# A convolution layer whose depthwise convolutions, statistics and element-wise work are laid out anew around the same matmuls

## Chip, cores and metric

One Trainium2 chip, 8 cores, the batch of 16 sequences split two to a core. The metric is the device time of the slowest core in microseconds (us), lower is better. Most executions agree within 0.3%, but an 8-core program also has a slower state in which the cores of one die run at a lower granted TensorE clock.

## The reference, cut to what matters

An encoder of four layers. Layer 1 has the convolution module below; every layer ends in a squared-ReLU MLP.

```python
def conv_module(h, w_in, dw, dw_bias, ln_g, ln_b, w_out):
    val, gate = jnp.split(h @ w_in, 2, axis=-1)
    v = val * jax.nn.sigmoid(gate)                   # (B, S, 1024), S = 2048
    v = depthwise_conv(v, dw, width=31) + dw_bias    # centred, per channel   (shortened)
    mu, var = mean(v), variance(v)                   # over the 1024 channels (shortened)
    vn = (v - mu) * lax.rsqrt(var + LN_EPS) * ln_g + ln_b
    return jax.nn.silu(vn) @ w_out

# ... for each layer i
    x = x + mixers[i](rms_norm(x, norm_mix[i]))
    x = x + sq_relu_mlp(rms_norm(x, norm_mlp[i]), mlp_up[i], mlp_down[i])
```

## The kernel before

A sequence of 2048 positions is cut into four tiles of 512 (`j` = 0 to 3) and the channels into eight chunks of 128 (`c`, or `oc` for outputs). All steps run on TensorE, including the depthwise convolution (32 narrow matmuls with diagonal weights for one chunk of one tile) and the sums over channels (a matmul with a matrix of ones). The matmuls of the trace follow the program's order (22,320 in both), so the order of the calls below is TensorE's schedule. The convolutions come as `conv(0..7)` for tile 0, `8..15` for tile 1, `16..23` for tile 3, `24..31` for tile 2.

```python
def ln_stats(j):                      # mean and reciprocal root of tile j (cut)
    if j > 1:
        flush(j)                      # the ones-matmuls of the tile's last chunks
        b1, b2 = S1, S2               # two fixed PSUM banks
    # ... tiles 0 and 1 use two free banks
    m, r = M[slot[j]], R[slot[j]]     # both in SBUF
    self.act(msq, b1, AF.Square)
    self.copy(m, b1, eng="act")
    self.tt(r, b2, msq, ALU.subtract)
    self.act(r, r, AF.Ln, bias=self.vcol("eps", 1))
    self.act(r, r, AF.Exp, scale=-0.5)

def ln(j, c, lag=2):                  # subtract the mean; two chunks later: scale, swish
    if c < DC:
        C = Cv(c, j)
        self.tt(C, C, M[slot[j]], ALU.subtract, eng="pool" if c % 2 or j == 2 else "dve")
        half.append((j, c))
    while half and (len(half) > lag or c >= DC):
        ln_end(*half.pop(0))

def ln_end(j, c):
    C = Cv(c, j)
    self.tt(C, C, R[slot[j]], ALU.mult)
    self.act(SLv(c, j), C, AF.Silu, bias=..., scale=...)

# ... out(j, oc): 8 matmuls, then x += bank on VectorE, squares on ScalarE for the next norm

for c in range(DC):                   # projection of tile 3
    glu(c, 3)
    if c < 4:
        out(0, 2 * c)
        out(0, 2 * c + 1)
    else:
        self.sq_flush()
    if c > 0:
        conv(7 + c)
    # ...
conv(15)
for c in range(DC):                   # tile 3's convolutions beside tile 1's normalization
    conv(16 + c)
    if c == 0:
        ln_stats(1)
    else:
        ln(1, c - 1)
for c in range(DC):                   # tile 2's convolutions
    conv(24 + c)
    if c == 0:
        ln(1, DC - 1)
        ln(1, DC)
    elif c == 1:
        ln_stats(3)
    else:
        ln(3, c - 2)
    if c % 2:
        out(1, c // 2)
# ... rest of tile 1's output, then tile 3's and tile 2's, each chunk beside ln() and the
# ... operands of the MLP's first products: hsteps() scales the residual (piece) and forms
# ... differences t1 to t4; slot_steps() forms three sums and a difference of weights
```

## Time and profile before

| | before |
|---|---|
| median of the first 3 runs | 4501.51 us (4497.52 to 4760.71) |
| profiled run, slowest core (core 2) | span 4496.5 us |
| spans of its 8 cores | 4476.3 to 4496.5 us, granted clock 0.990 to 0.993 |
| TensorE busy on core 2 | 4347.2 us of 4496.5 |

Two lines of the page's groups of instructions matter later (line, engine, operation, output and input, count, then busy us and mean ns of one, then the idle time before them):

```profile
L351 POOL TENSOR_TENSOR arena<-arena 128x512 f32<-128x512 f32 (+1 forms) x61 | 83.2, 1391 | 964.8 <-ACT arena L348 829.0
L366 DVE CAST arena<-arena 128x512 bf16<-128x512 f32 x32 | 20.4, 638 | 28.1 <-ACT arena L348 26.5
```

The first are GpSimd's subtractions. The second are VectorE's conversions of tiles 2 and 3 for the statistics; a mean of 638 ns hides two populations, which comes up at the end.

### The profile page before, as it was taken

The page shows a single profiled execution, that of the slowest core. Times are in us where ns is not written, and L with a number is a line of the kernel's source. Part 1 is how long each engine was busy: PE and PEld are TensorE (multiplying, and loading weights), DVE is VectorE, ACT ScalarE, POOL GpSimd, SP SyncE. Part 2 cuts the span into 40 slices and gives each one's busy share as a digit, 9 for nine tenths or more (in the row PEclk, how much of TensorE's full clock was granted, in tenths as well). Part 3 has the DMA queues.
Part 4 walks back from the last instruction along what each step waited for, and adds up shares of the span by engine and source line. Part 5 has one row for each costly group of instructions (what it writes and reads, how often), then busy time and mean ns, then how long its engine had stood idle before and what let it go on. Part 6 is the DMA issues. An engine that isn't in the chain of part 4 may idle for free.

```text
span 4496.5 us, 67459 instructions; the slowest of 8 cores (4476.3 to 4496.5 us)
## 1 busy us (share of the span) xinstructions
PE 4347.2 (97%) x22320; PEld 1959.2 (44%) x22320; DVE 2759.3 (61%) x5056; ACT 2020.6 (45%) x3452; POOL 162.7 (4%) x211
## 2 busy tenths in 40 slices
PE   7999999999999999999999999999999999999998
PEld 3444443444444444444444444434444444444443
DVE  2776645876767853677655656456646656426655
ACT  4443435543524445444354434454444344344434
POOL 0000001000010000000000000020000000000000
PEclk9999999999999999999999999999999999999999
DMA  6377755466646664366943445453443244412453
GB/s 158 88 166 197 194 109 123 105 151 206 179 122 158 178 193 128 71 161 194 245 153 108 153 150 148 100 131 115 148 157 143 75 159 150 166 52 101 149 186 132
DMA packets 122741, 652.31 MB, mean 145 GB/s; under 512 B 14624, under 2 KB 55712, under 8 KB 75552
## 3 DMA queue, kind: packets, MB, share of 16 engines
q1 hardware_dynamic: 102240, 517.46, 32.8%
q0 software_dynamic: 20160, 130.56, 16.8%
q8 instruction: 184, 3.01, 0.3%
q14 instruction: 157, 1.29, 0.1%
HBM read 625.35 MB, written 151.07 MB: 173 GB/s over the span
## 4 chain that ended last, share of the span: by engine, by line
PE 86%; DVE 6%; issue 3%; ACT 2%; DMA 2%; SPq 0%; DVEq 0%; POOL 0%; ACTq 0%; POOLq 0%
PE ps L334 86%; DVE arena L351 4%; ACT arena L348 2%; DVE arena L359 2%; DMA arena<-l_pool_w_in 1%; DMA outT<-arena 1%; DMA arena<-scr_v 0%; DMA arena<-scr_mlp 0%; DMA arena<-xT 0%; ACT L348 0%; DVE arena L355 0%; SPq L372 0%; DVEq L285 0%; POOL arena L372 0%; ACT ps L348 0%
## 5 line engine op out<-in xcount | busy, mean ns | idle before, releaser
L334 PE MATMUL ps<-arena 128*128 128x512 bf16 (+4 forms) x22320 | 4347.2, 371 | 131.6 <-ACT arena L348 49.8
L334 PEld LDWEIGHTS ps<-arena 128*128 128x128 bf16 (+1 forms) x22320 | 1959.2, 98 | 2519.1 <-issue 296.1
L351 DVE TENSOR_TENSOR arena<-arena,ps 128x512 f32<-128x512 f32 (+2 forms) x1026 | 721.7, 717 | 784.2 <-PE ps L334 778.1
L351 DVE TENSOR_TENSOR arena<-arena 128x512 bf16<-128x512 bf16 (+4 forms) x2318 | 1102.7, 493 | 161.2 <-ACT arena L348 125.9
L348 ACT ACTIVATE arena<-arena 128x512 bf16<-128x512 f32 (+4 forms) x1239 | 794.6, 652 | 545.4 <-DVE arena L351 513.5
L348 ACT ACTIVATE ps<-ps 128x512 f32<-128x512 f32 x770 | 448.1, 582 | 1100.4 <-PE ps L334 1038.7
L348 ACT ACTIVATE arena<-ps 128x512 f32<-128x512 f32 (+2 forms) x1114 | 614.3, 596 | 541.9 <-PE ps L334 505.0
L359 DVE SCALAR_TENSOR_TENSOR arena<-arena 128x512 bf16<-128x512 f32 (+1 forms) x944 | 666.0, 719 | 99.9 <-ACT arena L348 92.6
L351 DVE TENSOR_TENSOR arena<-ps,arena 128x512 f32<-128x512 f32 x520 | 357.4, 687 | 506.5 <-PE ps L334 474.5
L348 ACT ACTIVATE arena<-ps,arena 128x512 bf16<-128x512 f32 (+2 forms) x294 | 184.5, 664 | 240.2 <-PE ps L334 218.3
L351 POOL TENSOR_TENSOR arena<-arena 128x512 f32<-128x512 f32 (+1 forms) x61 | 83.2, 1391 | 964.8 <-ACT arena L348 829.0
L372 POOL DMA_DIRECT2D arena<-l_mlp x96 | 51.0, 532 | 1720.3 <-PE ps L334 1139.1
L359 DVE SCALAR_TENSOR_TENSOR arena<-arena,ps 128x512 bf16<-128x512 f32 (+1 forms) x75 | 51.2, 694 | 100.2 <-PE ps L334 74.2
L355 DVE TENSOR_SCALAR arena<-arena 128x512 bf16<-128x512 f32 (+1 forms) x112 | 46.5, 462 | 37.4 <-DMA arena<-xT 37.4
L348 ACT ACT_TABLE_LOAD x33 | 42.3, 1283 | 35.8 <-DMA arena<-xT 14.8
L366 DVE CAST arena<-arena 128x512 bf16<-128x512 f32 x32 | 20.4, 638 | 28.1 <-ACT arena L348 26.5
L372 POOL DMA_DIRECT2D arena<-l_conv_w_in x16 | 8.5, 533 | 593.9 <-DVE arena L351 533.1
L369 POOL MEMSET arena<- 128x1024 bf16 (+1 forms) x6 | 4.1, 722 | 471.4 <-DVE arena L351 471.4
L372 POOL DMA_DIRECT2D arena<-l_pool_w_in x14 | 7.6, 560 | 353.4 <-PE ps L334 352.5
L355 DVE TENSOR_SCALAR arena<-ps,arena 128x512 f32<-128x512 f32 x16 | 11.9, 746 | 1.0 <-PE ps L334 0.9
L366 DVE COPY arena<-arena 128x8 bf16<-128x8 bf16 (+1 forms) x10 | 4.0, 405 | 10.2 <-ACT arena L348 9.9
L372 POOL DMA_DIRECT2D arena<-l_conv_w_out x4 | 2.1, 530 | 133.0 <-PE ps L334 133.0
(10 smaller groups left out, 8.0 us busy)
## 6 DMA issues: line engine op xcount, KB each, us to landing
arena<-scr_mlp SPq DMA_DIRECT2D x160, 1792.0 KB, 7.3
scr_mlp<-arena SPq DMA_DIRECT2D x64, 1792.0 KB, 6.7
arena<-l_mlp POOLq DMA_DIRECT2D x96, 1024.0 KB, 8.9
arena<-scr_v SPq DMA_DIRECT2D x256, 130.0 KB, 3.8
arena<-xT SPq DMA_DIRECT2D x32, 512.0 KB, 7.9
outT<-arena SPq DMA_DIRECT2D x12, 1024.0 KB, 5.3
arena<-l_conv_w_in POOLq DMA_DIRECT2D x16, 512.0 KB, 8.4
scr_v<-arena SPq DMA_DIRECT2D x64, 128.0 KB, 2.3
```

The source lines that it names most:

```text
L334: self.P.add("pe", lambda e: e.matmul(out, lhsT, rhs, start=start, stop=stop, skip_group_check=skip), reads=[lhsT, rhs], writes=[out])
L348: self.P.add("act", lambda e: e.activation(out, in_, func, **kw), reads=reads, writes=[out])
L351: self.P.add(eng, lambda e: e.tensor_tensor(out, in0, in1, op), reads=[in0, in1], writes=[out])
L355: self.P.add(eng, lambda e: e.tensor_scalar(out, in0, s1, None, op0), reads=reads, writes=[out])
L359: self.P.add(eng, lambda e: e.scalar_tensor_tensor(out, in0, scalar, in1, op0, op1), reads=reads, writes=[out])
L366: self.P.add(eng, lambda e: e.tensor_copy(out, in_), reads=[in_], writes=[out])
L369: self.P.add(eng, lambda e: e.memset(ap, val), writes=[ap])
L372: return self.P.add(q, lambda e: e.dma_start(out=out, in_=in_), reads=[in_] + list(reads), writes=[out] + list(writes), chan=chan, group=g ...
```

## The change

The intent is to close the places where TensorE waits in the convolution layer. Four parts:

- **Order**: the projection loop of tile 3, which held most of tile 1's convolutions already, takes up to two convolutions a step, so that the first four of tile 3 fit in as well; statistics come earlier, outputs later; queues are one deeper. With it go new bank numbers and a new order of the operand differences behind the last output (the two `rest` lines).
- **Roots**: three reciprocal roots stay in PSUM banks instead of SBUF.
- **Subtractions**: the odd subtractions of tiles 0, 1 and 3 move from GpSimd to VectorE.
- **Tail**: four sums of weights (first sequence) and eight operand differences (each sequence) at the MLP's start move from VectorE to GpSimd.

```diff
-    def hsteps(self, n, pair, gp=()):
+    def hsteps(self, n, pair, gp=(), rs=None):
+        rs = rs or self.RS                     # piece() and root() now use rs[]
...
-        eng = "dve"                            # slot_steps: sums of weights
+        eng = "pool" if i == 0 and KINDS[li] == "conv" else "dve"
...
-        SB = [Rot([self.buf(b, BF16, (TT,), o + i * 1024) for i in range(4)]) for b, o in ((accb, 0), (sgb, 4096))]
+        SB = [Rot([self.buf(7, BF16, (TT,), o + i * 1024) for i in range(4)]) for o in (0, 4096)]
...
-                flush(keep=1)
+                flush(keep=2)
...
-            m, r = M[slot[j]], R[slot[j]]
+            m, r = M[slot[j]], S2 if j == 2 else R[slot[j]]
...
-                self.tt(C, C, M[slot[j]], ALU.subtract, eng="pool" if c % 2 or j == 2 else "dve")
+                self.tt(C, C, M[slot[j]], ALU.subtract, eng="pool" if j == 2 else "dve")
...
-            self.tt(C, C, R[slot[j]], ALU.mult)
+            self.tt(C, C, S2 if j == 2 else R[slot[j]], ALU.mult)
...
-            self.act(self.RS[1], S1, AF.Ln, bias=self.vcol("eps", 0))
-            self.act(self.RS[1], self.RS[1], AF.Exp, scale=-0.5)
+            self.act(S1, S1, AF.Ln, bias=self.vcol("eps", 0))
+            self.act(S1, S1, AF.Exp, scale=-0.5)
...
         for c in range(DC):
             glu(c, 3)
-            if c < 4:
-                out(0, 2 * c)
-                out(0, 2 * c + 1)
-            else:
+            for k in {0: (8,), 4: (15,), 5: (17,), 6: (), 7: (18, 19)}.get(c, (2 * c + 7, 2 * c + 8)):
+                conv(k)
+            if 1 <= c <= 4:
+                out(0, 2 * c - 2)
+                out(0, 2 * c - 1)
+            if c == 4:
+                ...
+                conv(16)
+            elif c == 5:
+                Cb[3] += self.take(9)
                 self.sq_flush()
-            if c > 0:
-                conv(7 + c)
...
-        for c in range(DC):
-            conv(16 + c)
-            if c == 0:
                 ln_stats(1)
-            else:
-                ln(1, c - 1)
+            elif c > 5:
+                for k in (0, 1) if c == 6 else (2, 3, 4, 5):
+                    ln(1, k)
+        for k in (20, 21, 22, 23):
+            conv(k)
+            if k < 23:
+                ln(1, k - 14)
...
         for c in range(DC):
             conv(24 + c)
             if c == 0:
-                ln(1, DC - 1)
-                ln(1, DC)
-            elif c == 1:
                 ln_stats(3)
-            else:
-                ln(3, c - 2)
-            if c % 2:
-                out(1, c // 2)
+            for k in range(c - 1, c) if c else ():
+                ln(3, k)
+            if c in (3, 5):
+                out(1, (c - 3) // 2)
...
+        ln(3, 7)
+        ln(3, DC)
+        out(1, 2)
+        out(1, 3)
+        ln_stats(2)
...
+        r0 = ps[:, 5, :]                       # root of the next norm, in PSUM
+        self.mm(r0, self.cm("ones", 128), nx.sums[0], True, True)
+        self.act(r0, r0, AF.Ln, bias=self.vcol("eps", 0))
+        self.act(r0, r0, AF.Exp, scale=-0.5)
-        for oc in range(5, DC):
+        for oc in range(4, DC):
             out(1, oc)
-            ln(3, oc + 1)
-        ln(3, DC)
-        self.h_open(nx)
+            for k in {4: (0, 1)}.get(oc, (oc - 3,)):
+                ln(2, k)
+        self.h_open(nx, (0, 1), (r0, S1))      # differences of chunks 0, 1 on GpSimd
...
-        rest = [root3] + [h[2 + 8 * k + q] for k in range(4) for q in range(2, 8)]
+        rest = [root3] + [h[2 + 8 * k + q] for k in range(2) for q in range(2, 8)]
+        rest += [h[2 + 8 * k + q] for qs in ((2, 3), (4,), (6,), (5,), (7,)) for k in (2, 3) for q in qs]
...
         for oc in range(DC):
             out(3, oc)
-            ln(2, oc)
-            first.pop(0)()
-        ln(2, DC)
-        self.mlp_sums(s, li)
+            if oc < 3:
+                ln(2, oc + 5)
+            elif oc == 3:
+                ln(2, DC)
+                self.mlp_sums(s, li)
+            else:
+                first.pop(0)()
+                first.pop(0)()
```

More of the change, by code (lines that the diff above doesn't have):

```diff
@@ L723, in load_chunk @@
             self.summed(n, j, n.sums[j])
-    def hsteps(self, n, pair, gp=()):
+    def hsteps(self, n, pair, gp=(), rs=None):
         ja, jb = pair
         h11, h21, h22, t3, t1, t2, t4 = [self.hview(i) for i in range(7)]
+        rs = rs or self.RS
         def piece(dst, kc, half, j, r):
             c = 4 * half + kc
-            self.stt(dst[:, kc, :], self.X[:, c, j * TT:(j + 1) * TT], self.vcol(n.gname, c), self.RS[r],
+            self.stt(dst[:, kc, :], self.X[:, c, j * TT:(j + 1) * TT], self.vcol(n.gname, c), rs[r],
                      ALU.mult, ALU.mult)
-        steps = [lambda: self.root(n, ja, self.RS[0]), lambda: self.root(n, jb, self.RS[1])]
+        steps = [lambda: self.root(n, ja, rs[0]), lambda: self.root(n, jb, rs[1])]
         for kc in range(4):
@@ L745, in hsteps, with h_open @@
         return steps
-    def h_open(self, n, gp=()):
+    def h_open(self, n, gp=(), rs=None):
         if self.hbuilt is not n and self.claim("H"):
             self.hbuilt = n
-            self.htodo = self.hsteps(n, self.pairs[0], gp)
+            self.htodo = self.hsteps(n, self.pairs[0], gp, rs)
     def h_step(self, k):
@@ L1357, in out @@
                 sq3.append((oc, t))
-                sq3_add(2)
+                sq3_add(3)
             if oc == DC - 1:
@@ L1397, in conv_layer @@
             glu(c, 3)
-            if c < 4:
-                out(0, 2 * c)
-                out(0, 2 * c + 1)
-            else:
-                self.sq_flush()
-            if c > 0:
-                conv(7 + c)
-            if c == 3:
-                self.take(slab[0])
-        conv(15)
-        self.rot = Rot([ps[:, i, :] for i in range(6)])
-        Cb[3] = self.take(8, 9)
-        for c in range(DC):
-            conv(16 + c)
-            if c == 0:
-                ln_stats(1)
-            else:
-                ln(1, c - 1)
+            if c == 2:
+                self.take(slab[0])
+            for k in {0: (8,), 4: (15,), 5: (17,), 6: (), 7: (18, 19)}.get(c, (2 * c + 7, 2 * c + 8)):
[4 more added lines that the diff above has]
+            if c == 4:
+                self.rot = Rot([ps[:, i, :] for i in range(6)])
+                Cb[3] = self.take(8)
+                self.take(7)
+                conv(16)
+            elif c == 5:
+                Cb[3] += self.take(9)
+                self.sq_flush()
+                ln_stats(1)
+            elif c > 5:
[5 more added lines that the diff above has]
+                ln(1, k - 14)
         Cb[2] = self.take(10, 15)
@@ L1419, in conv_layer @@
             if c == 0:
-                ln(1, DC - 1)
-                ln(1, DC)
-            elif c == 1:
                 ln_stats(3)
-            else:
-                ln(3, c - 2)
-            if c % 2:
-                out(1, c // 2)
+            for k in range(c - 1, c) if c else ():
+                ln(3, k)
+            if c in (3, 5):
+                out(1, (c - 3) // 2)
         self.release(dgb)
         self.release(v4)
-        self.slots_early(s, li, 2)
-        out(1, 4)
-        ln_stats(2)
-        self.rot = Rot([ps[:, i, :] for i in (0, 1, 2, 3, 4, 5, 7)])
-        for oc in range(5, DC):
+        ln(3, 7)
[3 more added lines that the diff above has]
+        ln_stats(2)
+        self.release(7)
+        self.slots_early(s, li, 2)
+        r0 = ps[:, 5, :]
+        self.rot = Rot([ps[:, i, :] for i in range(5)])
+        self.mm(r0, self.cm("ones", 128), nx.sums[0], True, True)
+        self.act(r0, r0, AF.Ln, bias=self.vcol("eps", 0))
+        self.act(r0, r0, AF.Exp, scale=-0.5)
+        for oc in range(4, DC):
             out(1, oc)
-            ln(3, oc + 1)
-        ln(3, DC)
-        self.h_open(nx)
+            for k in {4: (0, 1)}.get(oc, (oc - 3,)):
+                ln(2, k)
+        self.h_open(nx, (0, 1), (r0, S1))
         assert self.hbuilt is nx
         h, self.htodo = self.htodo, []
-        first = [h[0]] + [h[2 + 8 * k + q] for k in range(4) for q in range(2)]
-        rest = [root3] + [h[2 + 8 * k + q] for k in range(4) for q in range(2, 8)]
+        first = [h[2 + 8 * k + q] for k in range(4) for q in range(2)]
+        rest = [root3] + [h[2 + 8 * k + q] for k in range(2) for q in range(2, 8)]
+        rest += [h[2 + 8 * k + q] for qs in ((2, 3), (4,), (6,), (5,), (7,)) for k in (2, 3) for q in qs]
         for oc in range(DC):
             out(3, oc)
-            ln(2, oc)
-            first.pop(0)()
-        ln(2, DC)
-        self.mlp_sums(s, li)
-        self.htodo = first + rest
+            if oc < 3:
[6 more added lines that the diff above has]
+                first.pop(0)()
+        self.htodo = rest
+        self.rot = Rot([ps[:, i, :] for i in (2, 3, 4, 0, 7, 1, 5, 3)])
         for oc in range(DC):
@@ L1452, in conv_layer @@
             self.h_step(4)
-            if oc == 0:
-                self.rot = Rot([ps[:, i, :] for i in range(8)])
-                self.rot.i = 7
+        self.rot = Rot([ps[:, i, :] for i in range(8)])
         nx.lazy = [1, 2]
```

## The prediction

> **What bounds the kernel now.** I read the page from the top: busy times, then the chain of work that ended last.
>
> ```profile
> PE 4347.2 (97%) x22320; PEld 1959.2 (44%) x22320; DVE 2759.3 (61%) x5056; ACT 2020.6 (45%) x3452; POOL 162.7 (4%) x211
> ...
> PE 86%; DVE 6%; issue 3%; ACT 2%; DMA 2%; SPq 0%; DVEq 0%; POOL 0%; ACTq 0%; POOLq 0%
> ```
>
> TensorE is busy 97% of the span and is 86% of the chain. The change adds and removes no matmul, so all it can win is time in which TensorE stands still or runs at reduced clock: at most 4496.5 - 4347.2 = 149 us of idle time in the whole program, plus slow-clock time. The change touches only the convolution layer (run twice, once per sequence) and the start of the MLP behind it. So I asked the timeline of TensorE for that stretch. This is the first sequence, from the first depthwise convolution to the MLP (columns: start, us covered, then in brackets the idle time before it and what ended it):
>
> ```profile
> 603.50 64.10 PE L334 MATMUL ps<-arena 128*32 128x512 bf16 x471 [2.10 <-DMA arena<-scr_v]
> 667.93 0.38 PE L334 MATMUL ps<-arena 128*128 128x512 bf16 x1 [0.33 <-ACT arena L348]
> 670.78 56.91 PE L334 MATMUL ps<-arena 128*128 128x512 bf16 x458 [2.47 <-ACT arena L348]
> ...
> 735.79 15.55 PE L334 MATMUL ps<-arena 128*32 128x512 bf16 x209 [0.53 <-DMA arena<-scr_v]
> 753.58 0.38 PE L334 MATMUL ps<-arena 128*128 128x512 bf16 x1 [2.24 <-ACT arena L348]
> ...
> 786.86 0.38 PE L334 MATMUL ps<-arena 128*128 128x512 bf16 x1 [1.25 <-ACT arena L348]
> ...
> 790.61 17.66 PE L334 MATMUL ps<-arena 128*128 128x512 bf16 x69 [1.21 <-ACT arena L348]
> 809.46 0.38 PE L334 MATMUL ps<-arena 128*128 128x512 bf16 x1 [1.18 <-ACT arena L348]
> ...
> 829.28 1.13 PE L334 MATMUL ps<-arena 128*128 128x512 bf16 x4 [3.27 <-DVE arena L351]
> ```
>
> All matmuls have one source line, so I joined the trace to the program by order (22,320 matmuls in both). The gaps are then five places: at 668-671 the output projection of tile 0 waits for the swish of its own last chunks; at 753 tile 1's does; at 787-791 tile 3's; at 809-811 tile 2's; at 829 the MLP's first product waits for an operand difference that VectorE makes. The second sequence shows the same five.
>
> A gap also costs clock. The stretch table (busy us, count, then clock) shows it:
>
> ```profile
> 700.00:725.00 25.00, 25.00 (x248) 10.42 (x249) 9.36 (x16) 9.23 (x16) 0.00 (x0) 1.00 0.47 108
> ...
> 775.00:800.00 25.00, 21.21 (x85) 8.72 (x83) 17.87 (x22) 15.65 (x20) 13.91 (x10) 0.86 0.23 43
> 800.00:825.00 25.00, 22.63 (x105) 9.93 (x104) 23.45 (x41) 11.56 (x17) 0.58 (x1) 1.00 0.24 43
> ```
>
> 700-725 is the healthy state: TensorE full, VectorE at 9 of 25 us. At 775-800 TensorE is idle for 3.8 us and its clock is 0.86. At 800-825 VectorE is full (23.45 of 25): there it becomes the limit. The work of the layer is badly mixed: VectorE idles during the projections and is overloaded at the end.
>
> Last, why VectorE falls behind near 785. Its timeline and GpSimd's in the same 12 us:
>
> ```profile
> 782.01 2.53 DVE L351 TENSOR_TENSOR arena<-arena 128x512 f32<-128x512 f32 x2
> 784.46 0.67 DVE L351 TENSOR_TENSOR arena<-arena,ps 128x512 f32<-128x512 f32 x1
> ...
> 786.74 2.82 DVE L351 TENSOR_TENSOR arena<-arena 128x512 f32<-128x512 f32 x2
> ```
> ```profile
> 781.03 12.10 POOL L351 TENSOR_TENSOR arena<-arena 128x512 f32<-128x512 f32 x8 [3.74 <-DVE arena L351]
> ```
>
> While GpSimd works, VectorE's operations on two SBUF operands take 1.2 to 1.4 us each; the one with an operand in PSUM keeps its 0.67 us.
>
> **What the Trainium skill says.** "SBUF — State Buffer", Who interferes with whom: a VectorE instruction with two SBUF inputs contends with a GpSimd instruction that reads SBUF, one with at most one SBUF input does not. The fences above agree. "TensorE: Matmul & The Clock Gate", What's actually happening: after about one idle window of 3.4 us the clock is halved until a busy window has passed. The clock records here agree on the stretches (half clock for 3.41 or 6.83 us), but gaps of 2.2 us suffice in some places (755.0) and one of 2.47 us does not in another (2906), as the window runs free. "ScalarE: Activation LUTs", What ACT_TABLE_LOAD costs: 1283 ns per load; the trace has 1283 ns mean. "Perfetto Trace Analysis", Optimization Strategy: interleave regimes whose busiest engine differs, which is this change's idea.
>
> **The change, part by part.**
>
> *1. Convolutions spread over the gated projections.* Steady costs from the joined trace: a projection chunk (16 matmuls) 3.45 us, a convolution chunk (32 narrow ones) 1.92, an output chunk 1.73, a pair of statistics matmuls 0.43. In the loop over tile 3's projection each step now holds two convolutions of tile 1 and two output chunks of tile 0 (10.7 us of TensorE), for which ScalarE needs 0.6 + 2 x 1.3 + 2 x 0.63 = 4.5 us and VectorE 0.69 + 2 x 1.4 + 2 x 1.1 = 5.7. Both fit. Tile 0's output starts one step later, with one projection and three convolutions (9.2 us) in front of it, against a lateness of 5.2 us now (last swish at 671.3, first output chunk at 666.1): gap 1 goes. It costs 2.8 us idle (0.33 + 2.47) and 2.85 us from 6.83 us of half clock in sequence 1; 3.1 idle and no clock in sequence 2.
>
> *2. Tiles 1 and 3.* Statistics of tile 1 come inside the projection loop, so its swish is done about 6 us before its first output chunk; tile 3's is finished before two output chunks, the statistics and four more chunks, some 11 us of TensorE work. Gap 2: 2.9 idle + 1.7 clock, and 2.6 + 1.7. Gap 3: 3.8 + 2.5, and 4.6 + 2.7. Both go.
>
> *3. Tile 2.* Its subtractions stay on GpSimd (8 x about 1.3 us), but the reciprocal root stays in a PSUM bank, so VectorE's multiplications no longer meet GpSimd, and they begin four output chunks earlier. Gap 4: 2.4 and 2.4. It goes.
>
> *4. Subtractions of tiles 0, 1, 3 leave GpSimd.* 12 x 0.61 us (spacing) = 7.3 us more on VectorE per sequence, in stretches where it has room except one: from the end of the last projection through eight convolutions VectorE needs about 13.6 us and TensorE 13.7. The statistics of tile 3, now right after the first convolution of tile 2, flush three chunks at once and may wait for the last: I put 1.0 us of new gap per sequence.
>
> *5. The tail.* VectorE works without a break from 795 to 831.7, 36.6 us, beside 29.4 us of TensorE work (8 x 1.94 + 8 x 1.73). Moved off: 8 bf16 differences x 0.43 = 3.4; four slot sums of 1024 columns x 0.69 = 2.8 (first sequence only); 3 multiplications done earlier, 2.0. 36.6 - 8.2 = 28.4, so VectorE just fits. But the third tile's root comes only after the first output chunk of tile 2 plus a table load, and GpSimd's eight differences take 8 x 1.36 = 10.9 us (its bf16 mean) in series; they end about 2 us after the MLP could start, and VectorE's remaining differences (two SBUF inputs) meet them. Gap 5 shrinks from 3.6 + 1.7 clock (3.3 + 1.7) to about 1.7 us.
>
> *6. Small.* Two table loads fewer (9 to 7 from tile 1's statistics on), 2.6 us of ScalarE beside other work: 0. Flush and square queues one deeper: slack only. The convolution-input transfers that cost 0.53 and 0.40 us stay, as do the first convolution's 2.1 us.
>
> Sum before: sequence 1 5.65 + 4.6 + 6.3 + 2.4 + 5.3 = 24.2; sequence 2 3.1 + 4.3 + 7.3 + 2.4 + 5.0 = 22.1; together 46.3 us. Left after: 2 x (1.0 + 1.7 + 0.9 for one half-clock stretch in every second sequence) = 7.2. That is 39; I take off 3 for small waits that a reordering of this size brings. 36 us of 4501.5 gives 4465.
>
> **Rivals.**
> (a) VectorE becomes the bound in the dense convolution stretch (part 4). For it: 13.6 against 13.7 us leaves no slack, ScalarE is close too (12.8). Against it: queues are one deeper. Then each sequence loses 4 to 6 us, partly with half clock: 4475 to 4480.
> (b) GpSimd becomes the bound at the tail: slot sums (4 x about 2.7 us, an estimate as twice its 1.36 us for 512 columns) and eight differences in series, and weight loads that it issues queue behind them. For it: GpSimd needs about twice VectorE's time per element. Against: the sums start some 15 us before the differences. Then gap 5 stays as long as now: 4473.
> (c) All five gaps close wholly and the clock stays full: 4501.5 - 46 = 4455.
> (d) The stalls only move: tight back-to-back convolutions wait for their inputs (3.5 us median to landing, some 7 to 11 here). Then 4490.
>
> **Range and chances.** Mean of my own sum and the rivals weighted is near 4466. Runs of one kernel differ by some 0.1 to 0.3% (4497.5 and 4501.5; cores 4476 to 4497 in one run), or 5 to 13 us. I say 4465, 4450 to 4484. Even the whole 46 us is 1.0%, so faster by over 2% is out of reach: 0.01. Slower by over 2% would need 90 us of new waits in about 320 us of changed work: 0.01. Within 2%: 0.98.
>
> **What would show it.** Right: TensorE's timeline runs from tile 3's projection to the MLP with no gap over 1 us ended by ScalarE, clock at 1.0 there; each convolution layer about 18 us shorter; GpSimd's busy time about unchanged near 162 us (per sequence 12 subtractions of 1.40 us out, 8 differences of 1.36 us in, and once four slot sums); VectorE's multiplications of tile 2 at 0.68 us beside GpSimd. Wrong: a gap over 2 us in the dense convolution stretch ended by VectorE (rival a), one at the MLP's start ended by GpSimd (b), or more transfer waits (d). Were the layer's gaps gone but the time the same, the idea that these gaps lie on the path would be wrong.

## More of the kernel before

The `rest` lines matter for reading the experiments: the first product of the MLP that waits needs one of the 16 differences. In the old order 12 others come before it, in the new one 8.

## The result and the profile after

The changed kernel is correct. Its median is 4466.79 us over 13 runs (4452.51 to 5135.35), that of the kernel before 4501.51 us over 15 (4495.13 to 5118.64). The ratio of the fast runs is 0.9915 (95% interval 0.9904 to 0.9926). A ratio is the mean time of one kernel's fast runs over that of the other's of the same rounds, so it is not quite the ratio of the medians. Executions in which one die ran at a lower clock are left out of the means. The class is "same" (within 2%).

The page's busy times and chain of work after:

```profile
PE 4328.9 (97%) x22320; PEld 1957.8 (44%) x22320; DVE 2752.1 (62%) x5060; ACT 2013.6 (45%) x3448; POOL 153.9 (3%) x207
...
PE 87%; DVE 5%; DMA 3%; issue 2%; ACT 2%; SPq 0%; DVEq 0%; POOL 0%; ACTq 0%; POOLq 0%
```

TensorE has the same 22,320 matmuls and is 18.3 us less busy. That fits the clock: core 2's half-clock time in the two layers fell from 37.5 us to none, and half of 37.5 is 18.8. Its idle time on core 2 fell from 149.3 to 127.3 us (span minus busy). In the chain DMA went from 2 to 3%, a first hint of what is left. TensorE's timeline, first sequence, from the first depthwise convolution past the MLP's start:

```profile
602.71 127.42 PE L334 MATMUL ps<-arena 128*32 128x512 bf16 x1098 [0.34 <-DMA arena<-scr_v]
...
738.92 0.59 PE L334 MATMUL ps<-arena 128*128 128x512 bf16 x2 [0.54 <-DVE arena L366]
741.32 17.22 PE L334 MATMUL ps<-arena 128*128 128x512 bf16 x218 [1.80 <-DVE arena L366]
761.95 46.01 PE L334 MATMUL ps<-arena 128*32 128x512 bf16 x235 [3.41 <-DMA arena<-scr_v]
808.23 0.38 PE L334 MATMUL ps<-arena 128*128 128x512 bf16 x1 [0.27 <-DVE arena L351]
809.16 81.06 PE L334 MATMUL ps<-arena 128*128 128x512 bf16 x374 [0.56 <-DVE arena L351]
```

All waits for ScalarE's swish (the five gaps shown before) are gone. Three things are left. At 738.92 and 741.32 the statistics of tile 3 wait for the conversions (line 366) of its last two chunks. At 761.95 the last convolution waits 3.41 us for its input. The MLP starts after 0.27 + 0.56 us. Two of the stretches shown before:

```profile
775.00:800.00 25.00, 25.00 (x117) 11.37 (x116) 20.04 (x32) 15.20 (x21) 16.56 (x11) 1.00 0.00 1
800.00:825.00 25.00, 24.15 (x111) 10.49 (x109) 22.28 (x38) 11.34 (x20) 8.36 (x9) 1.00 0.49 122
```

The columns are as in the prediction: TensorE, its weight loads, VectorE, ScalarE and GpSimd, then clock. At 775-800 TensorE is now full at clock 1.00 (21.21 us at 0.86 before), with VectorE at 20 of 25 us and GpSimd at 16.6. Core 2, shown here, has no half-clock time left in these layers, but six of the eight cores still have some in the first sequence and six in the second; the table below has the mean.

For sizes below the noise of one core I use two measures. **Span**: the mean span of all undisturbed cores, that is of the dies on which all four cores kept a clock above 0.985, over all runs of a kernel (28 to 80 cores), minus the same for the kernel before in the same rounds. **Layer**: from the trace, the time from the first gated projection to 40 products into the MLP, both sequences added, as mean over the six cores whose trace holds all matmuls. The kernel before gave a mean span of 4485.0, 4485.1 and 4486.2 us in three sets of rounds and the changed kernel 4448.1 and 4448.0 in two, so the first repeats well. The two measures differ by up to 4.3 us for one kernel; I call nothing shown that is smaller and rests on one of them.

| per sequence (1, 2) | before | after |
|---|---|---|
| layer, us | 273.9, 273.0 | 254.7, 252.6 |
| TensorE idle in it, us | 17.0, 17.3 | 6.0, 4.2 |
| at half clock in it, us | 16.5, 14.2 | 2.8, 2.3 |

Half-clock time counts half. Idle plus half of that falls by 17.9 + 19.1 = 37 us, the layer by 39.6, the span by 37.0: within 3 us, the change acts only here, and by TensorE's waits and their clock.

### The profile page after: what moved, and what is told of

Its sections match the earlier page's. It is cut to its first block, busy times and chain, and to the rows that moved or that the text cites. A ratio compares the mean times of both kernels' runs of the same rounds, so it can differ in the third digit from the quotient of the medians.

```text
span 4456.2 us, 67424 instructions; the slowest of 8 cores (4437.8 to 4456.2 us)
## 1 busy us (share of the span) xinstructions
PE 4328.9 (97%) x22320; PEld 1957.8 (44%) x22320; DVE 2752.1 (62%) x5060; ACT 2013.6 (45%) x3448; POOL 153.9 (3%) x207
## 4 chain that ended last, share of the span: by engine, by line
PE 87%; DVE 5%; DMA 3%; issue 2%; ACT 2%; SPq 0%; DVEq 0%; POOL 0%; ACTq 0%; POOLq 0%
PE ps L334 87%; DVE arena L351 3%; DVE arena L359 2%; ACT arena L348 2%; DMA arena<-scr_v 1%; DMA outT<-arena 1%; DMA arena<-l_pool_w_in 1%; DMA scr_v<-arena 1%; DMA arena<-scr_mlp 0%; SPq L372 0%; DMA arena<-xT 0%; DVEq L285 0%; POOL arena L372 0%; ACT L348 0%; ACT ps L348 0%
## 5 line engine op out<-in xcount | busy, mean ns | idle before, releaser
L351 DVE TENSOR_TENSOR arena<-arena,ps 128x512 f32<-128x512 f32 (+2 forms) x1042 | 730.7, 716 | 764.3 <-PE ps L334 755.5
L351 DVE TENSOR_TENSOR arena<-arena 128x512 bf16<-128x512 bf16 (+5 forms) x2306 | 1091.7, 492 | 147.3 <-ACT arena L348 113.2
L348 ACT ACTIVATE arena<-arena 128x512 bf16<-128x512 f32 (+2 forms) x1231 | 790.3, 652 | 543.4 <-DVE arena L351 503.9
L359 DVE SCALAR_TENSOR_TENSOR arena<-arena 128x512 bf16<-128x512 f32 (+1 forms) x912 | 642.9, 719 | 97.6 <-ACT arena L348 89.4
L359 DVE SCALAR_TENSOR_TENSOR arena<-arena,ps 128x512 bf16<-128x512 f32 (+1 forms) x107 | 73.7, 707 | 110.8 <-PE ps L334 64.9
L351 POOL TENSOR_TENSOR arena<-arena 128x512 bf16<-128x512 bf16 (+2 forms) x57 | 74.6, 1330 | 881.9 <-ACT arena L348 724.5
L355 DVE TENSOR_SCALAR arena<-arena 128x512 bf16<-128x512 f32 (+1 forms) x112 | 46.5, 461 | 37.1 <-DMA arena<-xT 37.1
L366 DVE CAST arena<-arena 128x512 bf16<-128x512 f32 x32 | 13.7, 427 | 24.8 <-ACT arena L348 21.1
```

Source lines behind the costliest of these rows:

```text
L348: self.P.add("act", lambda e: e.activation(out, in_, func, **kw), reads=reads, writes=[out])
L351: self.P.add(eng, lambda e: e.tensor_tensor(out, in0, in1, op), reads=[in0, in1], writes=[out])
L355: self.P.add(eng, lambda e: e.tensor_scalar(out, in0, s1, None, op0), reads=reads, writes=[out])
L359: self.P.add(eng, lambda e: e.scalar_tensor_tensor(out, in0, scalar, in1, op0, op1), reads=reads, writes=[out])
L366: self.P.add(eng, lambda e: e.tensor_copy(out, in_), reads=[in_], writes=[out])
```

## The experiments

Twelve runs (one is the changed kernel again); all gave correct results. This is their outcome, explained one by one below. Differences are to the kernel before, in us.

| run | span | layer | ratio of fast runs (95%) |
|---|---|---|---|
| gap1_only | -8.9 | -5.9 | 0.9956 (0.9903 to 1.001) |
| engines_only | +3.1 | +5.0 | 0.9994 (0.9935 to 1.0054) |
| order_only | -35.1 | -39.4 | 0.9908 (0.9843 to 0.9973) |
| no_sub_move | -45.6 | -45.2 | 0.9876 (0.9808 to 0.9944) |
| changed_again | -37.1 | -40.8 | 0.9912 (0.9862 to 0.9963) |
| roots_and_tail_only | -7.3 | -5.9 | 0.9976 (0.9925 to 1.0026) |
| no_gpsimd_tail | -35.8 | -35.6 | 0.9905 (0.9864 to 0.9946) |
| no_psum_roots | -26.1 | -27.3 | 0.993 (0.9882 to 0.9978) |
| sub_move_only | +11.5 | +10.7 | 1.0023 (1.001 to 1.0037) |
| stats_later | -46.3 | -42.6 | 0.9895 (0.9878 to 0.9911) |
| no_sub_move_slot_held | -45.6 | -44.7 | 0.9897 (0.9882 to 0.9912) |
| no_sub_move_both | -47.2 | -48.1 | 0.9891 (0.9874 to 0.9907) |

The theory after the comparison was: the order makes the gain, because TensorE waited for swishes that now have other matmuls in front of them; the engine moves help only at the tail. Rivals: the engine moves make the gain by removing contention between VectorE and GpSimd, or the subtraction move costs something that the gain hides.

### gap1_only

```diff
-            if c < 4:
-                out(0, 2 * c)
-                out(0, 2 * c + 1)
-            else:
+            if 1 <= c <= 4:
+                out(0, 2 * c - 2)
+                out(0, 2 * c - 1)
+            elif c > 4:
                 self.sq_flush()
```

> The kernel before with one thing changed: the output chunks of tile 0 come one projection step later. If the gaps lie on the path and each is worth its idle time plus half of its half-clock time, this takes away the first gap alone: 2.8 us idle + 2.85 us of clock in the first sequence, 3.1 us in the second, so 6 to 9 us of the 4500 (ratio to before 0.998 to 0.9985), and the trace shows no gap over 0.5 us between tile 3's first projection chunk and the first output chunk, with the other four gaps as before. If a gap that is closed here only comes back later (the rival: the layer is bound by VectorE and ScalarE, not by the order), less than 2 us.

Tile 0's output one step later, in the old order. The wait of 2.8 to 3.1 us at tile 0's output falls to 0.33 in both sequences, and no other wait for a swish takes its place. But on two of the eight cores the next convolution of the first sequence waits 3.76 and 2.91 us for its input, where no gap over 0.5 us was expected. Span -8.9 us, layer -5.9, against 6 to 9 expected. So gaps of this kind are on the path, and their idle time and clock give the size to within 3 us.

### engines_only

The changed kernel's roots, subtractions and tail in the old order (all hunks of the diff but those of the order; the new order of the differences is in).

> The engine moves without the new order: the kernel before, with the roots of tile 2 and of the next norm kept in PSUM, the subtractions of tiles 0, 1 and 3 on VectorE, the slot sums and the differences of two chunks on GpSimd, and the tail of the differences reordered; the loops over convolutions and projections as before. My theory (order closes gaps 1 to 3, the engine moves close 4 and shrink 5): gaps 1, 2 stay, gap 3 shrinks, 4 and 5 mostly go: 10 to 18 us faster than before (ratio 0.996 to 0.998). The rival that the contention of VectorE and GpSimd is the cause of nearly all: 25 to 35 us faster (0.992 to 0.9945).

Missed by all that was expected: nothing was gained. The profiled run had four cores at clock 0.984, so I read only its waits; the layer figure in the table includes some of these cores and is +4.5 us on the other three (0, 1, 5). TensorE's timeline on core 7, first sequence:

```profile
780.35 0.38 PE L334 MATMUL ps<-arena 128*128 128x512 bf16 x1 [1.97 <-ACT arena L348]
782.42 0.58 PE L334 MATMUL ps<-arena 128*128 128x512 bf16 x1 [1.70 <-ACT arena L348]
...
822.91 67.46 PE L334 MATMUL ps<-arena 128*128 128x512 bf16 x311 [0.56 <-DVE arena L351]
```

The MLP's start is at 0.56 us, as wanted (3.4 to 3.5 us before), but tile 3's output now waits longer for its swish: 6.0 us in all over its eight input chunks, against 3.8 before (both first sequence). Tile 0's output waits 4.9 us instead of 3.0, tile 1's 3.4 instead of 2.5. One part gives and another takes. Which one takes is what the next runs had to tell.

### order_only

The changed kernel with roots in SBUF, odd subtractions on GpSimd and the tail on VectorE again (the reverse of the hunks above). It keeps the new order of the differences.

> The new order without the engine moves: the changed kernel with both roots back in SBUF, odd subtractions back on GpSimd, slot sums and differences back on VectorE. My theory: gaps 1 to 3 go, 4 mostly goes, 5 is back (some 3 us idle and a stretch of half clock per sequence, perhaps less as the order of the differences is kept): 25 to 33 us faster than before (ratio 0.9925 to 0.9945). Rival (contention is the cause): 5 to 15 us faster only, with gaps of 1 to 3 us ended by VectorE or ScalarE in the middle of the layer.

Order alone gives -35.1 us, nearly all of the -37.0. It also removes most of the last two gaps, which the prediction had credited to roots and tail: no wait of tile 2's output reaches 0.25 us (2.4 us in sum before), and the MLP's start 0.8 and 1.2 us instead of 3.5 and 3.4; in the first sequence 2.0 us of waits for the squares of tile 3's output (statistics of the next norm) come instead. TensorE's timeline on core 3, first sequence:

```profile
756.14 32.80 PE L334 MATMUL ps<-arena 128*32 128x512 bf16 x167 [2.68 <-DMA arena<-scr_v]
789.22 0.38 PE L334 MATMUL ps<-arena 128*128 128x512 bf16 x1 [0.28 <-ACT arena L348]
791.14 13.76 PE L334 MATMUL ps<-arena 128*128 128x512 bf16 x63 [1.54 <-ACT arena L348]
805.87 1.36 PE L334 MATMUL ps<-arena 128*128 128x512 bf16 x5 [0.97 <-DVE arena L351]
807.47 42.85 PE L334 MATMUL ps<-arena 128*128 128x512 bf16 x197 [0.24 <-DVE arena L351]
```

The two waits for ScalarE are for these squares, the two for VectorE are the MLP's start. How much of the shorter start comes from the loops and how much from the reordered differences is open: four differences fewer in front are about 4 x 0.43 = 1.7 us of VectorE (an estimate from the trace's 0.43 us each), against a fall of 2.2 to 2.7.

### no_sub_move

```diff
-                self.tt(C, C, M[slot[j]], ALU.subtract, eng="pool" if j == 2 else "dve")
+                self.tt(C, C, M[slot[j]], ALU.subtract, eng="pool" if c % 2 or j == 2 else "dve")
```

> The changed kernel with the odd subtractions of tiles 0, 1 and 3 back on GpSimd, nothing else. If the wait at the statistics of tile 3 (0.54 + 1.80 us in the first sequence, 1.72 in the second) is made by the 7.3 us that this move put on VectorE, it shrinks and the kernel is 2 to 4 us faster than the changed one. If GpSimd's slower subtraction (1.3 us against 0.6) and its hold on VectorE's two-SBUF-operand work cost more, the wait grows to 3 us and more, and the kernel is 2 to 10 us slower than the changed one (ratio to before 0.992 to 0.994).

This is the changed kernel with one line undone. It is faster than the changed kernel by 45.6 - 37.1 = 8.5 us (5.6 by the layer), more than the 2 to 4 expected. The wait for tile 3's statistics falls from 2.55 and 2.44 us to 1.8 and 0.9.

Against order_only, this kernel adds roots and tail together: 45.6 - 35.1 = 10.5 us more. So "35 of 37 by the order alone" hides two engine moves that nearly cancel, +10.5 and -8.5. The traces show how the subtraction move costs in the new order: in the changed kernel (core 2) the swishes of tile 1 come 1.2 us apart (727.50, 728.70, 729.91, 731.12), and VectorE then stands idle twice for 1.65 us, waiting for ScalarE. With the move undone (core 5) these swishes run in back-to-back pairs. sub_move_only below explains the pattern.

### changed_again

The changed kernel, unchanged, as the control.

> The changed kernel once more, as the control for the other runs of this chip. Every theory: mean span of the undisturbed cores 4448 us (a core counts if its die kept a granted clock above 0.985), against 4485 for the kernel before; ratio 0.991 to 0.992.

As expected: -37.1, mean span 4448.0 us.

### roots_and_tail_only

The kernel of engines_only with the subtractions back on GpSimd (the one-line diff of no_sub_move).

> The kernel before with the roots in PSUM and the tail work on GpSimd, but neither the new order nor the moved subtractions. Theory A (the subtraction move costs about 8 us wherever it is, and hid a gain of the other two parts in the run of all three engine parts): mean core span 4476 to 4480 against 4485 before, with the gap at the MLP's start under 1 us. Theory B (in the old order no engine part is worth anything, because the wait only moves forward to the swish of tile 3): 4484 to 4489.

Theory A: -7.3 us, mean span 4477.7, MLP start at 0.56 us. Tile 3's output waits 3.6 us, as before (3.8).

### sub_move_only

The kernel before with the one line the other way (the odd subtractions on VectorE).

> The kernel before with only the odd subtractions of tiles 0, 1 and 3 moved from GpSimd to VectorE. Theory A (the move lengthens each tile's own normalization chain, because subtraction and multiplication of every chunk are then on one engine, and costs the same in any order): mean span of undisturbed cores 4493 to 4497 against 4485 before, with the waits for the swish of tiles 0, 1 and 3 each 0.5 to 2 us longer and the MLP's start at 3.5 us as before. Theory B (it costs only together with the other parts): 4483 to 4487.

Theory A: +11.5 us, the only single part that makes the kernel slower beyond the interval. -7.3 + 11.5 = +4.2 fits engines_only (+3.1). How it costs can be read off ScalarE's timeline on core 3, at the end of tile 2's projection. Before:

```profile
654.36 0.81 ACT L348 ACTIVATE arena<-arena 128x512 bf16<-128x512 f32 x1 [1.55 <-DVE arena L351]
655.56 1.52 ACT L348 ACTIVATE arena<-arena 128x512 bf16<-128x512 f32 x2 [0.39 <-DVE arena L351]
656.98 0.57 ACT L348 ACTIVATE arena<-ps 128x512 f32<-128x512 f32 x1
```

With the subtractions moved:

```profile
652.94 0.81 ACT L348 ACTIVATE arena<-arena 128x512 bf16<-128x512 f32 x1 [2.23 <-DVE arena L351]
654.14 0.81 ACT L348 ACTIVATE arena<-arena 128x512 bf16<-128x512 f32 x1 [0.39 <-DVE arena L351]
655.34 0.81 ACT L348 ACTIVATE arena<-arena 128x512 bf16<-128x512 f32 x1 [0.39 <-DVE arena L351]
656.06 0.58 ACT L348 ACTIVATE arena<-ps 128x512 f32<-128x512 f32 x1
```

The 0.81 us instructions are swishes, the 0.57 us one that reads PSUM is the sigmoid of a projection chunk. Before, GpSimd had done all four odd subtractions ahead, as soon as the mean was there (643.79 to 648.73 in the same trace), and two swishes run back to back (x2). With both operations of every chunk on VectorE the swishes come 1.2 us apart, and the sigmoid, behind them in ScalarE's order, comes later: 5.9 instead of 4.1 us after its matmuls for that chunk, 7.2 instead of 4.9 for the last one. VectorE then waits for that sigmoid before it can go on. VectorE is not full; two engines wait for each other in turn. The waits for the swish of tiles 0, 1 and 3 grow from 3.0 to 5.1, 2.5 to 3.4 and 3.8 to 6.2 us (first sequence), those of tiles 0 and 3 a little more than the 0.5 to 2 us expected; half-clock time per layer grows from 16.5 to 23.9 us. The MLP's start was expected to stay at 3.5 us and fell to 2.2 and 2.5.

### no_gpsimd_tail

```diff
-        eng = "pool" if i == 0 and KINDS[li] == "conv" else "dve"
+        eng = "dve"
-        self.h_open(nx, (0, 1), (r0, S1))
+        self.h_open(nx, (), (r0, S1))
```

> The changed kernel with slot sums and all differences back on VectorE. Theory A (the tail is where VectorE is the limit, so 3.4 us of differences per sequence and 2.8 us of slot sums in the first show at the MLP's start): 4 to 8 us slower than the changed kernel, with a gap of 2 to 4 us ended by VectorE at the MLP's start. Theory B (the new order alone has freed VectorE enough): within 2 us of it.

By the span it is 1.3 us slower than the changed kernel (theory B), by the layer 4 to 5 us (theory A). The waits that show are 1.5 us for the last square of tile 3's output in the first sequence and 1.0 and 1.7 us at the MLP's first product, smaller than A's 2 to 4. The tail move helps by something between 1 and 5 us; these runs don't settle it more closely. The reordered differences are in this run too.

### no_psum_roots

```diff
-            m, r = M[slot[j]], S2 if j == 2 else R[slot[j]]
+            m, r = M[slot[j]], R[slot[j]]
-            self.act(S1, S1, AF.Ln, bias=self.vcol("eps", 0))
-            self.act(S1, S1, AF.Exp, scale=-0.5)
+            self.act(self.RS[1], S1, AF.Ln, bias=self.vcol("eps", 0))
+            self.act(self.RS[1], self.RS[1], AF.Exp, scale=-0.5)
... (the same for r0 and for the multiplication in ln_end)
```

> The changed kernel with the reciprocal roots back in SBUF. Theory A (two SBUF operands beside GpSimd cost VectorE 0.6 us more in each of tile 2's 8 multiplications and 8 scalings, about 5 to 9 us per sequence, of which some lies on the path): 3 to 8 us slower than the changed kernel, tile 2's multiplications at about 1.3 us. Theory B (hidden behind the four earlier starts of the new order): within 2 us, with the same 1.3 us.

More than theory A's range: 10.9 us slower than the changed kernel. VectorE's timeline on core 3 tells why. Without roots in PSUM:

```profile
773.23 1.17 DVE L351 TENSOR_TENSOR arena<-arena 128x512 f32<-128x512 f32 x1
774.32 0.68 DVE L351 TENSOR_TENSOR arena<-arena,ps 128x512 f32<-128x512 f32 x1
774.92 4.55 DVE L351 TENSOR_TENSOR arena<-arena 128x512 f32<-128x512 f32 x2
779.39 0.67 DVE L351 TENSOR_TENSOR arena<-arena,ps 128x512 f32<-128x512 f32 x1
779.99 4.54 DVE L359 SCALAR_TENSOR_TENSOR arena<-arena 128x512 bf16<-128x512 f32 x2
```

The same operations in the changed kernel:

```profile
780.84 2.63 DVE L351 TENSOR_TENSOR arena<-arena,ps 128x512 f32<-128x512 f32 x4 [0.44 <-PE ps L334]
783.39 1.40 DVE L359 SCALAR_TENSOR_TENSOR arena<-arena,ps 128x512 bf16<-128x512 f32 x2
```

Beside GpSimd's subtractions a multiplication of two SBUF operands takes 1.17 us. At 774.92 and 779.99 GpSimd has come to the sums of weights (1024 columns, 2.4 to 2.6 us each here), and each such VectorE instruction takes about 2.3 us. With one operand in PSUM it is 0.68 to 0.74 in the same company. So VectorE finishes tile 3's output late, the matmuls that sum its last squares wait 5.6 us in the first sequence (mean of six cores), and the MLP starts 1.0 and 3.1 us late instead of 0.8 and 0.6. Each of the four slow instructions ends 0.55 to 0.56 us after one of GpSimd's sums ended (776.94 after 776.39, 779.47 after 778.92, and so on), as if it had stood still until then.

The sums explain the larger part, not all: they run in the first sequence only, and by the layer 8.2 of the 12.3 us lost there are in the first. In the second the scalings beside GpSimd's differences take 1.04 to 1.4 us instead of 0.74. Sums and differences belong to the tail part: beside the roots in PSUM their cost does not arise, and in order_only, with neither, it does not either.

### stats_later

```diff
-            if c == 0:
+            if c == 1:
                 ln_stats(3)
-            for k in range(c - 1, c) if c else ():
-                ln(3, k)
+            if c > 1:
+                ln(3, c - 2)
...
+        ln(3, 6)
         ln(3, 7)
```

> The changed kernel with tile 3's statistics two convolutions into tile 2's block instead of one. Theory A (the two waits of about 2.5 us per sequence come only from flushing tile 3's last two chunks right behind their convolutions): they go, no wait takes their place, mean core span 4443 to 4446 against 4448 of the changed kernel. Theory B (VectorE is full there and the wait moves to a later chunk or to tile 3's output): 4447 to 4450, with a new wait of 1 to 3 us ended by ScalarE or VectorE.

The changed kernel with tile 3's statistics one convolution later. TensorE's timeline on core 3:

```profile
639.81 85.92 PE L334 MATMUL ps<-arena 128*128 128x512 bf16 x745
727.41 22.64 PE L334 MATMUL ps<-arena 128*32 128x512 bf16 x288 [1.68 <-DMA arena<-scr_v]
750.42 46.02 PE L334 MATMUL ps<-arena 128*32 128x512 bf16 x235 [0.37 <-DMA arena<-scr_v]
796.71 0.38 PE L334 MATMUL ps<-arena 128*128 128x512 bf16 x1 [0.26 <-DVE arena L351]
```

The waits for line 366 are nearly gone (0.4 us mean of six cores, from 2.5) and none for VectorE or ScalarE has come in place. Theory A, and larger than expected by the span: 9.2 us faster than the changed kernel; by the layer 3.0 us (1.8 against changed_again's). In this profiled run two cores waited nearly 3 us for the last convolution's input, which raises the layer's mean.

### no_sub_move_slot_held

```diff
     def slot_load(self, s, li, i, after=()):
-            self.dma("pool", ..., self.wdram[f"l{li}_mlp"][g])
+            self.dma("pool", ..., self.wdram[f"l{li}_mlp"][g], writes=list(after))
...
-        self.slots_early(s, li, 2)
+        self.slots_early(s, li, 2, (dg(DC - 1),))      # on top of no_sub_move
```

> The changed kernel with the odd subtractions on GpSimd again, and the first 1 MB weight load held until the last convolution has read its diagonal, so that it can't run beside that convolution's input transfer. Theory A (the weight load slows that transfer): the wait before the last convolution of the first sequence, 1.2 us mean over the cores and up to 3.4, falls under 0.4, mean core span 4436 to 4438 against 4439.4 with the subtractions alone undone. Theory B (the transfer is late for another reason): the wait stays at 1 us or more, 4438 to 4441.

In the changed kernel's trace the 3.41 us wait for the last convolution's input has a neighbour: GpSimd issues the first 1 MB weight load of the MLP at 747.97 us, and the four reads of that input (130 KB each) are issued at 748.0 to 749.3 and land at 755.1 to 761.8. Both were waiting for the same earlier convolution. It happens in the first sequence only, as does this load. With the load held back the wait falls from 1.2 us mean to under 0.25 on all six cores, so the mechanism is theory A's. The total missed: 4440.6 us, not 4436 to 4438. The first sequence's layer is 1.8 us shorter than with no_sub_move; the second's is 2.3 longer, with 1.7 us of waiting for its first convolution's input, which this edit doesn't touch.

### no_sub_move_both

Both edits above on top of no_sub_move.

> Subtractions on GpSimd again, weight load held, and tile 3's statistics one convolution later: all that the earlier runs point to. If the three are independent: 4432 to 4436 mean core span, ratio to before 0.9885 to 0.990, the layer's idle time about 2 us per sequence. If GpSimd's subtractions of tile 3 then run beside VectorE's at a worse place: 4437 to 4441.

TensorE's timeline on core 6, the slowest:

```profile
639.89 94.26 PE L334 MATMUL ps<-arena 128*32 128x512 bf16 x830
735.46 7.15 PE L334 MATMUL ps<-arena 128*32 128x512 bf16 x102 [1.31 <-DMA arena<-scr_v]
742.79 59.38 PE L334 MATMUL ps<-arena 128*32 128x512 bf16 x388 [0.19 <-DMA arena<-scr_v]
802.73 57.53 PE L334 MATMUL ps<-arena 128*128 128x512 bf16 x265 [0.56 <-DVE arena L351]
```

The layer has 1.9 and 2.2 us of idle time left and no half clock on any of the six cores: 249.2 and 249.6 us. By waits, the edits are independent, and the worse place for GpSimd's subtractions, which the expectation offered as the reason for a smaller gain, does not show: TensorE waits for VectorE only 0.56 us, at the MLP's start. By the span (4439.1 us) they are not: no_sub_move, stats_later and both together lie within 1.6 us of each other in their gain, where independent gains would have made both clearly better than either. A part of that is plain: undoing the subtraction move and delaying the statistics remove the same wait. How the rest is spread can't be told from spans at 1 to 2 us. This version beats both kernels: ratio 0.9891 to the kernel before, fast runs 4444.25 to 4445.1 us against 4451.1 to 4478.07 of the changed kernel in both its sets.

## Why the prediction was right, and where not

The total was right (4465 against 4466.79; range 4450 to 4484). In the terms of its sum: 36 us predicted, 37 measured as idle plus half-clock time. That the fast-run gain is the ratio's 0.85%, some 38 us, says the same. But this close agreement is luck: 46.3 us of waits and clock were counted before and 49.6 measured, 7.2 + 3 us expected to be left and 12.7 measured, and the two errors cancelled.

- **Part 1, gap 1: right.** 5.65 + 3.1 = 8.75 us predicted; alone it gave 8.9 by the span, 5.9 by the layer. The clock share was read from core 2 alone and differs by core: in the first sequence 6.83 us at half clock on three cores, 3.41 on two, none on three; in the second, where none was predicted, five cores have 3.41 to 6.83.
- **Part 2, gaps 2 and 3: right.** Both are gone in order_only and in the changed kernel.
- **Part 3, gap 4: right that it goes, wrong in who removes it.** The output of tile 2 no longer waits in order_only either, with the root in SBUF. The durations were right (0.68 us with the root in PSUM). What the roots are worth, 10.9 us, is not gap 4 (4.8 us predicted): it is what the sums of weights (by the layer about two thirds) and the differences on GpSimd would otherwise do to VectorE. The prediction saw the differences meet VectorE's work, but not the sums.
- **Part 4, the subtractions: the mis-sized term.** 1.0 us of new gap per sequence was put at the right place, the statistics of tile 3, and the right cause, the last chunks' flush. It measured 2.5 us idle per sequence plus half-clock time; undoing the move returns 5.6 to 8.5 us in all. The reasoning counted VectorE's load (13.6 us of 13.7) and not the order in which VectorE and ScalarE wait for each other. In the old order, where VectorE had room, the same move cost 11.5 us, and swishes 1.2 us apart stand in the changed kernel's trace as well. Rival (a) named the stretch and the form (4 to 6 us per sequence, partly at half clock); with 2.8 (layer) to 4.3 us (span) per sequence the truth lies near or below its lower end. Its total of 4475 to 4480 was 2 to 3 us too high for its own terms (4465 + 8 to 12).
- **Part 5, the tail: right in direction.** 1.7 us predicted, 0.8 and 0.6 measured. The differences took 1.15 us each on GpSimd instead of 1.36, the sums 2.13 instead of 2.7; rival (b) did not come. VectorE was not without a break in the kernel before, as part 5 had it: at 797.4 and 815.2 it stands still for 0.88 and 0.93 us. Most of the credit for the shorter start belongs to the order, the reordered differences included, which no run separates.
- **Part 6: one thing changed that was to stay.** The input of the last convolution now costs 1.4 us on average in the first sequence and 3.41 on core 2 (rival (d) in one place), because a weight load starts with it.
- **What would show it:** no gap over 1 us ended by ScalarE, and layers shorter by 19 and 20 us (about 18 predicted), held. Clock 1.00 held on core 2, the one profiled before and after, and not on most others: the mean is 2.8 and 2.3 us at half clock per layer. GpSimd's busy time was to stay near 162 us and fell to 153.9; with the durations measured, 24 x 1.39 out, 16 x 1.15 and 4 x 2.13 in, 6.5 us of the 8.8 are explained; nearly all of the rest is that the subtractions which stayed took 1.27 us instead of 1.40.

Not settled: the tail part's worth (1 or 4 to 5 us), what the new order of the differences does by itself, and whether the last edits add in full.

## What to carry to other kernels

Find the matmul that waits, and put other ready matmuls in front of it: order alone gave 35 of 37 us here. Measure every engine move beside it on its own: here a good one (10.5 us in the new order) and a bad one (8.5) looked like nothing together, and without the bad one the gain was 45.6. In this kernel an engine with idle time was not free to take work, because it and a second engine wait for each other in turn: what counts is how late the chain's last link comes, not the busy share. Before work moves to GpSimd, check what VectorE does in that time; keeping one of its two operands in PSUM was worth 10.9 us here.

## What the Trainium skill lacked or had wrong

- "SBUF — State Buffer", Who interferes with whom: right that two SBUF operands contend with GpSimd, and that the one who loses blocks until the other is done, but without a time for it. Here 0.68 us became 1.17 beside GpSimd instructions of 512 columns (which went from 1.27 to 1.72 us themselves) and about 2.3 us beside those of 1024 columns, each ending 0.55 us after the GpSimd instruction; 0.68 with an operand in PSUM. The page also lists `cast`, which reads one operand, among the operations that can contend with GpSimd when they run in a 2-port mode, which my prediction left out: in the kernel before VectorE's casts took 0.43 us alone and 1.45 to 1.82 beside GpSimd, and with the change the 32 of them have a mean of 427 ns, as the page would lead one to expect.
- "TensorE: Matmul & The Clock Gate", What's actually happening: it says one idle window of about 3.4 us, and not how much idle time inside a window is enough. Here a single gap of 1.80 us was followed by half clock (no_sub_move, core 3, at 734.0), while gaps of 0.33 and 2.48 us in a row were not (before, core 1, at 661 to 665). The half-clock stretches were 3.41 or 6.83 us long, in three of the runs also 10.24.
- No page that I read has it: moving one of a chunk's two operations to an engine that was less than half busy there (VectorE, 11.7 of 25 us at 650 to 675 in the kernel before, core 2) delayed a sigmoid on a third engine from 4.9 to 7.2 us and cost 11.5 us.
- No page that I read has a size for it: a 1 MB load issued with a 130 KB read; the read's last part was issued at 749.3 and landed 12.5 us later, against a median of 3.4 for this buffer's transfers.
